# Query-key products placed behind the products with values, a full-height sample chunk, and one tile of high and low parts for the samples' output projection

## The chip, the cores and the metric

The kernel runs on one core of a Trainium2 chip. The metric is device time in microseconds (us), the median of several runs. The core has a matrix engine (TensorE, "PE" in the rows; "PEld" is its loading of weights), VectorE (DVE), ScalarE (ACT), GpSimd (POOL), and queues of memory transfers that are issued by SyncE (SP). The engines run side by side and wait for each other through semaphores. TensorE writes into PSUM, which has eight banks of 128 x 512 float32; the other engines read the results from there into the on-chip memory.

## The reference

One layer of a hybrid decoder trunk, for a prompt of 1024 tokens and for samples (8 sequences of 8 tokens, 64 tokens in all), all in float32:

```python
h = rmsnorm(x) * (1 + scale) + shift              # adaLN, from c
q, k, v, g_att, z, xbc, dt, g_a, g_b = split(h @ w_in)
for window, dilation in ((128, 1), (512, 4), (2048, 16)):
    o, lse = dilated_window_attention(q, k, v)    # 8 heads of 64, ALiBi; samples read a cache
att = combine(o, lse) * silu(g_att)
y = gated_rmsnorm(ssd(conv(xbc), dt) + d_skip * x, z)   # 32 heads of 64, state 128, chunks of 128
merged = sigmoid(g_a) * (att @ w_att_branch) + sigmoid(g_b) * (y @ w_ssm_branch)
out = rmsnorm(x + gate * (merged @ w_out))
```

It returns the new rows, the kept keys and values, and the states of the scan and of the convolution.

## The kernel before

Activations lie transposed (features on the partitions, 1088 tokens along them: 1024 of the prompt and then 64 of the samples). To keep float32 accuracy, the large products are made of three: an operand is split into a high part of type F32R and a low part (what is left), and a product is high x high, low x high and high x low (`mm3`, lines 195 to 200; `pj` in the rows is a PSUM tile of such a projection, of 352 or 368 columns).

The work has four stages. First come norm, modulation and two early projections. Then come the attention, the state-space branch, and the output.

In attention and state-space branch the order of TensorE's instructions is the order in which the program writes them. The projections are the main stream (`run`), and the attention or the scan is a second stream (`attention`, `side`), a generator that is advanced between groups of projection products whenever its due time by a running estimate has come (`order.spend`, `yield`). So each step of the attention is a short burst of products between projection products. The other engines' order is set by a scheduler when the kernel is built. In the output stage that scheduler also orders TensorE.

The attention of a prompt group (`prompt_group`, lines 590 to 679) works on a pair of heads at a time: head 0 on partitions 0 to 63, head 1 on partitions 64 to 127. There are 12 such groups (4 pairs of heads, 3 dilations). A group has `nb` blocks of queries, 4 for the first two dilations and 2 for the third. For each block there is

- `scores`: the query-key products into two PSUM tiles `s0`, `s1` (rows `s<-k,q`). They use 64 rows of the matrix engine, the two heads side by side (form `64*128` in the rows). Then VectorE adds the mask and takes the extreme value into `pr` (line 617), and ScalarE takes the exponent (line 620);
- `turned`: transposes of `pr` (rows `pt`, full array, form `128*128`), copied to `pT` by ScalarE and VectorE (lines 639, 641);
- `values`: products of `pT` with the values (rows `o<-pT,v`), 64 columns of the array for each head (form `128*64`).

A step `i` of the loop at line 663 issues `values(i - 2)`, then `turned(i - 1)`, then `scores(i)`. `pr` has one buffer; the two PSUM tiles of scores have two banks in all.

In the state-space branch (`x_tile`), the products within a chunk (`yd`, lines 1074 to 1084) run over eight chunks of 128 tokens and a ninth, of the 64 sample tokens, that uses 64 rows (form `64*64`). The mask `CB`, with which the decays `mt` are multiplied, has zeros on partitions 64 to 127 of the samples' columns already (line 937).

In the output stage (lines 1105 to 1223), the branches' products add up in `acc`; for each of the 8 feature blocks `m` the merged result is split into `mhi[m]` and `mlo[m]` (`split`). `ada_gate` makes the adaLN gate from eight tiles `wg`, which lie in the pool `yw`. The last loop, over `t`, takes 128 tokens at a time and the 64 samples as `t == 8`. For each half of the features (quarter for the samples) it makes 8 x 3 products into a bank (`fo`), and then VectorE multiplies by the gate and adds the residual (lines 1209, 1210), ScalarE sums the squares (1211), and VectorE multiplies by the norm's weight (1212). After the last part come the norm's factor and the store.

Of the kernel before, what the change touches and what calls it, by code (L numbers as in the profile page):

```python
# [9 lines left out]
F32 = mybir.dt.float32  # L10
F32R = mybir.dt.float32r
AF = mybir.ActivationFunctionType
OP = mybir.AluOpType
# [3 lines left out]
D = 1024  # L17
T = 1024
NB = 8
NS = 8  # L20
TS = NB * NS
TT = T + TS
KO = D // 128
# [87 lines left out]
def trunk(ctx: ExitStack, tc: tile.TileContext, I, O):  # L111
    nc = tc.nc
    V, S, G, PE, SP = nc.vector, nc.scalar, nc.gpsimd, nc.tensor, nc.sync
# [18 lines left out]
    bankA, bankB, bankC, bankPJ = bank("a"), bank("b"), bank("c"), bank("p")  # L132
# [73 lines left out]
    def mm(out, w, x, ns, **kw):  # L206
        PE.matmul(out, w, x, **kw)  # L207
        order.spend(ns)
# [248 lines left out]
        del gates[:n]  # L457
        return [job(j) for j in js]

    def ada_gate(pool_, k, pg):  # L460

        wg = pool_.tile([128, D], F32, tag="wg", name="wg", bufs=1)
        SP.dma_start(out=wg, in_=I["w_gate"][k])
        for j in range(4):
            PE.matmul(pg[j * 32:j * 32 + 32, :256], scT[:, k, :], wg[:, j * 256:(j + 1) * 256], start=k == 0, stop=k == 7)
        if k < 7:
            return
        gt = pool_.tile([128, 256], F32, tag="gt", name="gt", bufs=1)
        for j in range(4):
            SP.dma_start(out=gt[j * 32:j * 32 + 32], in_=bass.AP(tensor=I["b_gate"].tensor, offset=I["b_gate"].offset + j * 256,  # L470
                                                                 ap=[[0, 32], [1, 256]]))
        V.tensor_add(gt, gt, pg[:, :256])
        for j in range(4):
            SP.dma_start(out=gate_d[:, j * 256:(j + 1) * 256], in_=gt[j * 32:j * 32 + 9])
# [8 lines left out]
    with ExitStack() as actx:  # L483
# [106 lines left out]
        def prompt_group(hp, g, n, q, k, v, msk, o):  # L590


            w = 256 if g < 2 else 128
            per = 512 // w
            nb = 8 // per
            st = ap_.tile([128, 2, 2, 8], F32, tag="st", name="st")
            prs, pTs, pos = {}, {}, {}

            def behind(u):
                return 2 if (g == 0 and u > 0) or (g == 1 and u % 2 == 1) else 1  # L600

            def scores(i):
                us = range(i * per, i * per + per)

                ps = [bankA("s0"), bankA("s1")]
                for u in us:
                    nkb = behind(u)
                    c0, k0 = (u - us[0]) * w, (u + 1 - nkb) * 128
                    for h in range(2):
                        hs = slice(h * 64, h * 64 + 64)  # L610
                        mm(ps[h][:, c0:c0 + nkb * 128], q[hs, u * 128:(u + 1) * 128], k[hs, k0:k0 + nkb * 128], 110.0 * nkb,
                           start=True, stop=True)
                pr = prs[i] = ap_.tile([128, 2, 512], F32, tag="pr", name="pr", bufs=1)
                for u in us:
                    c0, m = (u - us[0]) * w, behind(u) * 128
                    for h in range(2):
                        V.tensor_tensor_reduce(out=pr[:, h, c0:c0 + m], in0=ps[h][:, c0:c0 + m], in1=msk[:, h, w - m:w],  # L617
                                               scale=-1.0, scalar=3e38, op0=OP.add, op1=OP.min,
                                               accum_out=st[:, 0, h, u:u + 1])
                        S.activation(pr[:, h, c0:c0 + m], pr[:, h, c0:c0 + m], AF.Exp, scale=-1.0,  # L620
                                     bias=st[:, 0, h, u:u + 1], accum_out=st[:, 1, h, u:u + 1])

            def turned(i):
                pr = prs.pop(i)
                pT = pTs[i] = ap_.tile([128, 8, 128], F32, tag="pT", name="pT", bufs=1)
                us = range(i * per, i * per + per)
                half = per // 2
                for x in range(2):
                    pt = bankB("pt").rearrange("p (x n) -> p x n", n=128)
                    y = 0  # L630
                    for u in us[x * half:x * half + half]:
                        nkb = behind(u)
                        for h in range(2):
                            for b in range(nkb):
                                c0 = (u - us[0]) * w + b * 128
                                turn(pt[:, y, :], pr[:, h, c0:c0 + 128], ident)
                                y += 1
                    if x:
                        V.tensor_copy(pT[:, 4:4 + y], pt[:, :y])  # L639
                    else:  # L640
                        S.activation(pT[:, :y], pt[:, :y], AF.Copy)

            def values(i):
                pT = pTs.pop(i)
                us = range(i * per, i * per + per)
                half = per // 2
                for x in range(2):
                    y = 4 * x
                    for u in us[x * half:x * half + half]:
                        if u % 4 == 0:  # L650
                            pos[0] = bankC("o")
                        po = pos[0]
                        nkb = behind(u)
                        for h in range(2):
                            for b in range(nkb):
                                mm(po[h * 64:h * 64 + 64, (u % 4) * 128:(u % 4 + 1) * 128],
                                   v[:, u + 1 - nkb + b, h * 64:h * 64 + 64], pT[:, y, :], 115.0,
                                   start=b == 0, stop=b == nkb - 1)
                                y += 1
                        if u % 4 == 3:  # L660
                            S.activation(o[:, (u - 3) * 128:(u + 1) * 128], po, AF.Copy)

            for i in range(nb + 2):
                if i > 1:
                    values(i - 2)
                if 0 < i <= nb:
                    turned(i - 1)
                if i < nb:
                    scores(i)
                if i == nb - 1:  # L670
                    order.passed.add(("s", n))
                if i <= nb:
                    order.spend(300)
                    yield (5500.0 if g < 2 else 7500.0),
            ps = bankB("stt")
            turn(ps[:32, :128], st.rearrange("p a h u -> p (a h u)"), ident)
            sr = ap_.tile([32, 128], F32, tag="sr", name="sr", bufs=1)
            V.tensor_copy(sr, ps[:32, :128])
            SP.dma_start(out=st_d[hp, g].rearrange("a h (u n) -> (a h u) n", n=128), in_=sr)
# [146 lines left out]
    with ExitStack() as bctx:  # L826
# [135 lines left out]
        def x_tile(gr, xt, Bk, Bs, CB, CT, CS, sq):  # L962
# [111 lines left out]
            for q in range(3):  # L1074
                ps = bankA("yd")
                w = 512 if q < 2 else TS
                if q == 2:
                    yield 2000.0,
                for c in range(4 * q, 4 * q + 4 if q < 2 else 9):
                    n = 128 if c < 8 else TS  # L1080
                    for h in range(2):
                        mm(ps[h * 64:h * 64 + 64, (c % 4) * 128:(c % 4) * 128 + n],
                           xdt[:n, c, h * 64:h * 64 + 64], mt[h][:n, c * 128:c * 128 + n], 115.0, start=True, stop=True)
                V.tensor_add(u[:, 512 * q:512 * q + w], u[:, 512 * q:512 * q + w], ps[:, :w])
            zs = tiles.pop(("z", xt))
            th = b1.tile([128, TT], F32, tag="ecs", name="th")
# [21 lines left out]
    with pool("yr", 2) as yr, pool("yw", 2) as yw:  # L1108
# [31 lines left out]
        for gr in range(5):  # L1140
# [9 lines left out]
            for m in range(8):  # L1150
                vhi, vlo, _ = load_w(I["w_ssm"][gr, m] if gr < 4 else I["w_att"][m], 4, 128, yw)
                if gr == 1:
                    ada_gate(yw, m, pg)
                if gr == 3:
                    raw = yr.tile([128, D], F32, tag="yx", name="wo")
                    SP.dma_start(out=raw, in_=I["w_out"][m])
# [19 lines left out]
                if gr == 4:  # L1176
# [2 lines left out]
                    mhi.append(a)  # L1179
                    mlo.append(b)  # L1180


    fp = ctx.enter_context(pool("fin", 1))
    f2 = ctx.enter_context(pool("fin2", 2))
# [6 lines left out]
    for t in range(9):  # L1191
# [6 lines left out]
        m = 2 if t < 8 else 4  # L1198
        w = D // m
        for i in range(m):  # L1200
            ps = bankA("fo")[:n, :w]
            cs = slice(i * w, (i + 1) * w)
            for k in range(KO):
                hi = mhi[k][:, t * 128:t * 128 + n]
                lo = mlo[k][:, t * 128:t * 128 + n]
                PE.matmul(ps, hi, whi[:, k, cs], start=k == 0, stop=False)  # L1206
                PE.matmul(ps, lo, whi[:, k, cs], start=False, stop=False)  # L1207
                PE.matmul(ps, hi, wlo[:, k, cs], start=False, stop=k == KO - 1)  # L1208
            V.tensor_tensor(y[:n, cs], ps, (gbs if t == 8 else gb)[:n, cs], op=OP.mult)
            V.tensor_tensor(y[:n, cs], y[:n, cs], x[:n, cs], op=OP.add)  # L1210
            S.activation(ps, y[:n, cs], AF.Square, accum_out=s[:n, 3 + i:4 + i])
            V.tensor_tensor(x[:n, cs], y[:n, cs], fg[:n, cs], op=OP.mult)
# [158 lines left out]
```

## Time and profile before

| | |
|---|---|
| median of 3 runs | 1911.06 us (1909.26 to 1911.51) |
| the profiled execution | 1912.37 us, its span 1910.6 us |
| TensorE busy | 1871.7 us (98% of the span) |
| VectorE busy | 1023.6 us (54%) |
| ScalarE busy | 665.1 us (35%) |
| GpSimd busy | 359.7 us (19%) |
| mean granted TensorE clock | 0.992 |

The span is the time from the first to the last instruction of the profiled execution. In the timelines a row is a run of equal instructions: start in us from the span's start, length in us, engine, line, operation, output<-inputs, the form and how often. Products are pipelined, and their lengths overlap; what tells the pace is the distance from one start to the next.

### The profile page before, as it was taken

To read this page: it belongs to the slowest core of one execution; us is meant where nothing else is said; L and a number is where in the kernel's file an instruction comes from. 1 tells how busy PE (TensorE), PEld (TensorE's weight loads), DVE (VectorE), ACT (ScalarE), POOL (GpSimd) and SP (SyncE) were. 2 spreads that over 40 slices of the span, in tenths; PEclk is the share of its full clock that TensorE was granted. 3 is DMA by queue.
4 is the path that set the end of the run, shared out by engine and by line. 5 is a ranking of instruction groups with operands and counts; after the bars stand their busy time and mean duration, and the time that the engine had idled before them with its cause. 6 is when DMAs were issued, how large, how long until landed. Compare 5 with 4: busy or idle time off the path is not lost.

```text
span 1910.6 us, 32219 instructions
## 1 busy us (share of the span) xinstructions
PE 1871.7 (98%) x13057; PEld 1747.7 (91%) x13057; DVE 1023.6 (54%) x1946; ACT 665.1 (35%) x1275; POOL 359.7 (19%) x576
## 2 busy tenths in 40 slices
PE   6999999999999999999999999999999999999998
PEld 4999989988998999999989998999898999999987
DVE  4633343325324322566675777577757666566654
ACT  4444233313423332424343435243434332131222
POOL 3100000000000000134513442444244300001300
PEclk8999999999999999999999999999999999999999
DMA  8422462273246227434443444444233364364322
GB/s 331 140 79 93 156 205 77 86 227 121 97 158 197 84 90 242 149 124 170 147 140 132 155 151 137 138 140 135 86 104 104 120 236 143 124 198 144 120 89 78
DMA packets 108949, 269.57 MB, mean 141 GB/s; under 512 B 41580, under 2 KB 50592, under 8 KB 105536
## 3 DMA queue, kind: packets, MB, share of 16 engines
q1 hardware_dynamic: 108800, 267.51, 42.3%
q8 instruction: 102, 1.67, 0.4%
q14 instruction: 47, 0.39, 0.1%
HBM read 224.93 MB, written 80.26 MB: 160 GB/s over the span
## 4 chain that ended last, share of the span: by engine, by line
PE 87%; DVE 5%; DMA 4%; ACT 2%; issue 1%; POOL 1%; SPq 0%; ACTq 0%; POOLq 0%; DVEq 0%
PE pj L198 22%; PE pj L199 21%; PE pj L200 21%; PE o L207 2%; PE pt L211 2%; PE s L207 2%; PE fo L1208 2%; PE fo L1206 2%; PE fo L1207 2%; PE yo L207 2%; DMA csb<-cs_d 2%; PE yd L207 2%; PE early L242 1%; PE stt L207 1%; PE tt L211 1%
## 5 line engine op out<-in xcount | busy, mean ns | idle before, releaser
L198 PE MATMUL pj<-h_hi,whi 128*128 128x368 f32 x2256 | 753.4, 334 | 0.0
L199 PE MATMUL pj<-h_hi,wlo 128*128 128x368 f32 x2256 | 738.4, 327 | 0.0
L200 PE MATMUL pj<-h_lo,whi 128*128 128x368 f32 x2256 | 738.4, 327 | 0.0
L198 PEld LDWEIGHTS pj<-h_hi,whi 128*128 128x128 f32 x2256 | 424.3, 188 | 25.5 <-issue 23.0
L199 PEld LDWEIGHTS pj<-h_hi,wlo 128*128 128x128 f32 x2256 | 424.6, 188 | 0.7
L200 PEld LDWEIGHTS pj<-h_lo,whi 128*128 128x128 f32 x2256 | 424.1, 188 | 0.0
L192 DVE TENSOR_TENSOR wlo<-wraw,whi 128x1024 fp32r<-128x1024 f32 (+1 forms) x136 | 151.0, 1110 | 204.9 <-ACT whi L191 203.0
L191 ACT ACTIVATE whi<-wraw 128x1024 fp32r<-128x1024 f32 (+1 forms) x136 | 126.5, 930 | 326.8 <-PE pj L200 262.5
L198 PE MATMUL pj<-yhi,whi 128*128 128x368 f32 (+1 forms) x480 | 157.7, 329 | 0.7 <-DVE acc L1170 0.7
L199 PE MATMUL pj<-yhi,wlo 128*128 128x368 f32 (+1 forms) x480 | 157.2, 327 | 0.0
L200 PE MATMUL pj<-ylo,whi 128*128 128x368 f32 (+1 forms) x480 | 156.9, 327 | 0.0
L620 ACT ACTIVATE pr<-pr,st 128x128 f32<-128x128 f32 (+1 forms) x192 | 83.9, 438 | 69.0 <-DVE st L617 68.9
L639 DVE COPY pT<-pt 128x512 f32<-128x512 f32 x40 | 27.6, 690 | 137.6 <-PE pt L211 64.0
L198 PEld LDWEIGHTS pj<-yhi,whi 128*128 128x128 f32 x480 | 90.1, 188 | 3.7 <-issue 2.1
L199 PEld LDWEIGHTS pj<-yhi,wlo 128*128 128x128 f32 x480 | 90.1, 188 | 1.5 <-issue 0.8
L200 PEld LDWEIGHTS pj<-ylo,whi 128*128 128x128 f32 x480 | 90.1, 188 | 0.0
L874 DVE SCALAR_TENSOR_TENSOR xc<-raw,cw,xc 128x1112 f32<-128x1112 f32 x60 | 82.5, 1375 | 12.3 <-ACT xc L872 11.5
L559 POOL COPY ks<-k 128x64 f32<-128x64 f32 x12 | 3.7, 306 | 379.2 <-DVE k L500 379.2
L1175 POOL TENSOR_TENSOR acc<-acc,ta 128x368 f32<-128x368 f32 (+1 forms) x24 | 24.2, 1009 | 249.2 <-DVE ta L1174 249.2
L969 DVE TENSOR_TENSOR csb<-tok,csb 128x2048 f32<-128x2048 f32 x16 | 39.6, 2477 | 55.3 <-DMA csb<-cs_d 55.3
L1002 POOL TENSOR_TENSOR xde<-xdt,tok 128x256 f32<-128x256 f32 x64 | 45.3, 734 | 115.9 <-DVE xdt L995 115.9
L500 DVE COPY k<-pj 128x368 f32<-128x368 f32 (+2 forms) x44 | 24.0, 581 | 75.0 <-PE pj L200 72.5
(269 smaller groups left out, 2596.6 us busy)
## 6 DMA issues: line engine op xcount, KB each, us to landing
wraw<-in_w_in SPq DMA_DIRECT2D x96, 512.0 KB, 4.4
csb<-cs_d SPq DMA_DIRECT2D x16, 1088.0 KB
kt<-in_kc SPq DMA_DIRECT2D x32, 448.0 KB, 4.6
out_kc<-in_kc SPq DMA_DIRECT2D x32, 448.0 KB, 5.0
out_vc<-in_vc SPq DMA_DIRECT2D x28, 512.0 KB, 4.7
vt<-in_vc SPq DMA_DIRECT2D x28, 512.0 KB, 5.5
sg_d<-sg SPq DMA_DIRECT2D x16, 544.0 KB, 2.7
ecs<-cs_d SPq DMA_DIRECT2D x32, 272.0 KB, 3.9
```

Of the source, the lines that this page charges most:

```text
L191: S.activation(hi, raw, AF.Copy)
L192: V.tensor_sub(lo, raw, hi.bitcast(F32))
L198: PE.matmul(ps, whi[:, k, :], xhi[k], start=first and k == 0, stop=False)
L199: PE.matmul(ps, wlo[:, k, :], xhi[k], start=False, stop=False)
L200: PE.matmul(ps, whi[:, k, :], xlo[k], start=False, stop=last and k == n - 1)
L207: PE.matmul(out, w, x, **kw)
L211: PE.transpose(out, x, eye)
L620: S.activation(pr[:, h, c0:c0 + m], pr[:, h, c0:c0 + m], AF.Exp, scale=-1.0, bias=st[:, 0, h, u:u + 1], accum_out=st[:, 1, h, u:u + 1])
L874: V.scalar_tensor_tensor(c, raw[:, t:t + CONV], cw[:, j, t:t + 1], c, op0=OP.mult, op1=OP.add)
L969: V.tensor_tensor(csb[:, :, :T].rearrange("p h (c l) -> p h c l", l=CH), tok[:, :8, 32 + h0:34 + h0].rearrange("p c h -> p h c")[:, :, :, ...
L1002: G.tensor_tensor(xde[:, c:c + 2].rearrange("p c (h d) -> p c h d", h=2), xdt[:, c:c + 2, :].rearrange("p c (h d) -> p c h d", h=2), tok[: ...
L1206: PE.matmul(ps, hi, whi[:, k, cs], start=k == 0, stop=False)
```

## The change

Three edits.

1. In `prompt_group`, `scores` is cut in two: the products stay in `scores`, and the mask, the extreme value and the exponents become `exponents`. A step now issues `values(i - 2)`, `scores(i)`, `turned(i - 1)`, `exponents(i)`.
2. In `x_tile`, the ninth chunk of `yd` uses all 128 rows; the upper 64 rows of `mt` hold zeros there.
3. In the output stage, the samples' columns of `mhi[m]` and `mlo[m]` are copied side by side into a tile `smp` (128 x 8 x 128) by ScalarE. For `t == 8`, eight products of `smp` with the high part of the weights give high x high on PSUM partitions 0 to 63 and low x high on partitions 64 to 127. ScalarE copies the latter to `low`, VectorE multiplies it by the gate and adds it to the residual `x`. Eight more products, of the high part with the low part of the weights, add to partitions 0 to 63. `smp` shares its place with `wg`, which moves from the pool `yw` to the pool `acp`.

```diff
-    def ada_gate(pool_, k, pg):
+    def ada_gate(pool_, wgp, k, pg):
-        wg = pool_.tile([128, D], F32, tag="wg", name="wg", bufs=1)
+        wg = wgp.tile([128, D], F32, tag="smp", name="wg")
...
-                ps = [bankA("s0"), bankA("s1")]
+                ps = sps[i] = [bankA("s0"), bankA("s1")]
...
+            def exponents(i):
+                us = range(i * per, i * per + per)
+                ps = sps.pop(i)
                 pr = prs[i] = ap_.tile([128, 2, 512], F32, tag="pr", name="pr", bufs=1)
...
             for i in range(nb + 2):
                 if i > 1:
                     values(i - 2)
+                if i < nb:
+                    scores(i)
                 if 0 < i <= nb:
                     turned(i - 1)
                 if i < nb:
-                    scores(i)
+                    exponents(i)
...
                         mm(ps[h * 64:h * 64 + 64, (c % 4) * 128:(c % 4) * 128 + n],
-                           xdt[:n, c, h * 64:h * 64 + 64], mt[h][:n, c * 128:c * 128 + n], 115.0, start=True, stop=True)
+                           xdt[:, c, h * 64:h * 64 + 64], mt[h][:, c * 128:c * 128 + n], 115.0, start=True, stop=True)
...
-                    ada_gate(yw, m, pg)
+                    ada_gate(yw, acp, m, pg)
...
+                    if m == 0:
+                        smp = acp.tile([128, KO, 2 * TS], F32R, tag="smp", name="smp")
+                    S.activation(smp[:, m, :TS], a[:, T:].bitcast(F32), AF.Copy)
+                    S.activation(smp[:, m, TS:], b[:, T:].bitcast(F32), AF.Copy)
...
-            ps = bankA("fo")[:n, :w]
+            ps = bankA("fo")
             cs = slice(i * w, (i + 1) * w)
-            for k in range(KO):
+            if t == 8:
+                for k in range(KO):
+                    PE.matmul(ps[:, :w], smp[:, k, :], whi[:, k, cs], start=k == 0, stop=k == KO - 1)
+                low = f2.tile([TS, w], F32, tag="low", name="low")
+                S.activation(low, ps[TS:, :w], AF.Copy)
+                V.tensor_tensor(low, low, gbs[:, cs], op=OP.mult)
+                V.tensor_tensor(x[:n, cs], x[:n, cs], low, op=OP.add)
+                for k in range(KO):
+                    PE.matmul(ps[:n, :w], smp[:, k, :TS], wlo[:, k, cs], start=False, stop=k == KO - 1,
+                              skip_group_check=True)
+            ps = ps[:n, :w]
+            for k in range(KO if t < 8 else 0):
```

More of the change, by code (lines that the diff above doesn't have):

```diff
@@ L596, in prompt_group @@
             st = ap_.tile([128, 2, 2, 8], F32, tag="st", name="st")
-            prs, pTs, pos = {}, {}, {}
+            sps, prs, pTs, pos = {}, {}, {}, {}
             def behind(u):
```

## The prediction

> **What bounds the kernel now.** I read the page first (engines, chain), then TensorE's waits, then its groups with the shapes kept apart, then timelines of single bursts.
>
> ```profile
> span 1910.6 us, 32219 instructions
> PE 1871.7 (98%) x13057; PEld 1747.7 (91%) x13057; DVE 1023.6 (54%) x1946; ACT 665.1 (35%) x1275; POOL 359.7 (19%) x576
> PE 87%; DVE 5%; DMA 4%; ACT 2%; issue 1%; POOL 1%; SPq 0%; ACTq 0%; POOLq 0%; DVEq 0%
> PE pt L211 <- ACT pr L620: 2.7, 3, 1.0
> PE cb L207 <- DVE CT L881: 2.5, 1, 2.5
> ```
>
> TensorE is busy for 98% of the span and holds 87% of the chain, so whatever shortens its stream ahead of the last stage moves the end. The waits named for it are small; the one on `pr` is touched by this change. "Busy" hides pace, though: lengths overlap, and a slower start-to-start distance inside a busy stretch is seen only in a timeline. This is one full step of the attention between projection products:
>
> ```profile
> 100.93 0.33 PE L200 MATMUL pj<-h_lo,whi 128*128 128x368 f32 x1
> 101.19 0.93 PE L207 MATMUL o<-pT,v 128*64 128x128 f32 x12
> 102.05 1.09 PE L211 MATMUL pt<-pack,pr 128*128 128x128 f32 x8
> 103.07 1.13 PE L207 MATMUL s<-k,q 64*128 64x256 f32 x8
> 104.14 0.44 PE L198 MATMUL pj<-h_hi,whi 128*128 128x368 f32 x1
> 104.41 0.33 PE L199 MATMUL pj<-h_hi,wlo 128*128 128x368 f32 x1
> 104.58 0.33 PE L200 MATMUL pj<-h_lo,whi 128*128 128x368 f32 x1
> ...
> 109.88 1.15 PE L207 MATMUL o<-pT,v 128*64 128x128 f32 x16
> 110.96 1.09 PE L211 MATMUL pt<-pack,pr 128*128 128x128 f32 x8
> ```
>
> The step uses three shapes of the array: 64 columns per head (`o`), the full array (`pt`), 64 rows (`s`), and then the full array again. Their paces: two projection starts in a row are 0.17 us apart (104.41, 104.58). Four more `o` make 1.08 instead of 0.86 us, so twelve should take 0.66. Two more bursts give the other paces:
>
> ```profile
> 760.59 0.33 PE L200 MATMUL pj<-h_lo,whi 128*128 128x368 f32 x1
> 760.76 0.39 PE L211 MATMUL soT<-pack,so 128*128 128x128 f32 x2
> 760.90 0.41 PE L198 MATMUL pj<-h_hi,whi 128*128 128x368 f32 x1
> 761.15 0.33 PE L199 MATMUL pj<-h_hi,wlo 128*128 128x368 f32 x1
> ...
> 143.93 0.33 PE L200 MATMUL pj<-h_lo,whi 128*128 128x368 f32 x1
> 144.10 0.82 PE L211 MATMUL pt<-pack,pr 128*128 128x128 f32 x6
> 144.84 0.93 PE L207 MATMUL s<-k,q 64*128 64x128 f32 x8
> 145.70 0.43 PE L198 MATMUL pj<-h_hi,whi 128*128 128x352 f32 x1
> 145.97 0.32 PE L199 MATMUL pj<-h_hi,wlo 128*128 128x352 f32 x1
> ```
>
> Two transposes between projections take 761.15 - 760.59 = 0.56 us with two projection paces (0.34) in it, thus 0.11 each, and nothing for going to them and back: both are full array. The `s` at 144.84 have four records of 128 columns (the row merges both shapes) and take 0.86 us; all eight of 256 columns take 1.07. Doubling two pairs adds 0.21, so a pair of heads takes 0.105 us per 128 columns. Now the full step, from 100.93 to 104.58: 3.65 us, of which 0.50 are three projection paces, 0.66 `o`, 0.88 `pt`, 0.84 `s`. The 0.77 us left are four changes of shape, 0.19 each.
>
> **The change part by part.** *Scores ahead of the transposes.* The step becomes projection, `o`, `s`, `pt`, projection; from `pt` back to projections no shape changes. Four changes become three. This holds where a step has all three, at i = 2 and 3 of the two dilations with four blocks: 4 for each pair of heads, 16 in all: 16 x 0.19 = 3.1 us. No row shows `o` followed directly by `s`. If the direct change costs what the two that it replaces cost (0.38), the gain is 0; if it were free, 6.2. I take the mean of the four that are shown.
>
> At i = 1 there are `pt` and `s` alone (three per pair of heads, 12 in all). From 143.93 to 145.97 are 2.04 us: two projection paces 0.33, six `pt` 0.66, `s` 0.63, and 0.42 for two changes. After there are two as well, into `s` and from `s` to `pt`, and the projection's late second start (0.27 for 0.17 us) goes; `pt` behind another shape loses a little less (1.02 - 0.88 = 0.14 on both of its sides together). I take 0.04 each, 0.5 us, with 0 to 1.3 as bounds.
>
> *Waits in these steps.* The dearest wait on `pr` is in the first steps behind a combination of heads:
>
> ```profile
> 437.26 0.27 PE L211 MATMUL pt<-pack,pr 128*128 128x128 f32 x1
> 437.59 0.41 DVE L617 CUSTOM_DVE_ANT_0 pr<-s,msk 128x256 f32<-128x256 f32 x1
> 438.53 0.93 PE L211 MATMUL pt<-pack,pr 128*128 128x128 f32 x5 [1.00 <-ACT pr L620]
> ```
>
> TensorE loses 1.27 - 0.11 = 1.16 us here. With `s` in front it will wait for something else: both score banks must be free, which is when VectorE's last reduction ends, 437.59 + 0.41 = 438.00, so 0.74 is lost and 0.42 gained; the exponents end under the new `s`. Of three such places (2.7 us in the waits view) I take 1.0 us together, bounds 0 and 2.7. In the other steps scores now come at the place where `pt` stood and need the reductions only, which end ahead of the exponents. The new order delays the exponents: `pr` is free only behind the last transpose, and VectorE copies `pT` first. But `pt` comes later by the 1.07 us of `s`, so nobody waits longer; the evacuations of projections queued behind them on ScalarE and VectorE move by under 1 us against three projection banks that TensorE takes 24 x 0.17 = 4.1 us each to fill. Cost 0. No transfer is moved.
>
> *The ninth chunk at full height.* Two pairs of products per tile, 16 tiles:
>
> ```profile
> 889.81 0.33 PE L207 MATMUL yd<-csb,xdt 64*64 64x64 f32 x4
> 890.07 0.43 PE L198 MATMUL pj<-h_hi,whi 128*128 128x368 f32 x1
> ...
> 810.90 0.33 PE L207 MATMUL cb<-CTs,xcs 128*64 128x64 f32 x2
> 811.16 0.44 PE L198 MATMUL pj<-h_hi,whi 128*128 128x368 f32 x1
> ```
>
> The shape goes from `64*64` to `128*64`, still not that of the projections on both sides, so two changes stay two. 128 rows and 64 columns (`cb`) end as soon behind their start (0.26 us) as the low form. I take 0, bounds 0.8 us either way (16 x 0.05). The zeros are there already, so no instruction is added.
>
> *The samples' output projection.* 96 products become 64:
>
> ```profile
> 1891.20 0.28 PE L1206 MATMUL fo<-wohi,yhi 128*64 128x256 f32 x1
> 1891.40 0.69 DVE L1209 TENSOR_TENSOR fy<-fo,gb 128x512 f32<-128x512 f32 x1 [3.46 <-PE fo L1208]
> 1895.15 0.42 DVE L1212 TENSOR_TENSOR fx<-fy,fg 64x256 f32<-64x256 f32 x1
> 1895.50 0.15 DVE L158 TENSOR_TENSOR fs<-fs 128x1 f32<-128x1 f32 x1
> 1896.06 0.49 DVE L1222 TENSOR_SCALAR fy<-fx,fs 128x512 f32<-128x512 f32 x1
> 1902.50 0.28 PE L1208 MATMUL fo<-wolo,yhi 128*64 128x256 f32 x1
> 1902.83 0.42 DVE L1209 TENSOR_TENSOR fy<-fo,gbs 64x256 f32<-64x256 f32 x1 [1.27 <-PE fo L1208]
> 1903.28 0.42 DVE L1210 TENSOR_TENSOR fy<-fy,fx 64x256 f32<-64x256 f32 x1
> ```
>
> 95 distances from 1891.20 to 1902.50 are 0.119 us each, so 32 products fewer are 3.8 us of TensorE. But VectorE gets eight more operations of 64x256, in a stage where it was waiting for TensorE only 1.27 us a quarter. Ahead of the last residual addition (1903.28) it has, counted from 1891.40: what is left of `t == 7` (three of 0.7 and one of 0.49, seven small ones), two small sums, and ten, now eighteen, of 64x256. An independent one follows after 0.35 us (1895.15 to 1895.50), a dependent one after 0.45 (1902.83 to 1903.28). With 0.35: 2.15 + 0.49 + 9 x 0.12 + 18 x 0.35 = 10.0, so 1901.4 instead of 1903.28: 1.9 us gained. With 0.45 throughout: 11.8, gain nil. If TensorE alone set the end: 3.8. VectorE has two quarters' work to interleave, so I take 1.9. The second eight products must wait if they may not write while ScalarE reads the same bank; the next quarter's first eight stand ready to fill that.
>
> The Trainium skill, page "TensorEngine Tiling (Array Packing)", section "PSUM Bottleneck", says that packing speeds up the matrix engine and not the emptying of PSUM. By that rule the tail gains what VectorE allows (sum 6.5 us below); by TensorE's pace alone the sum would be 8.4. The row's 1.27 us of VectorE idling per quarter against eight added operations agrees with the rule.
>
> *Copies into `smp`.* Sixteen on ScalarE, of 128x64:
>
> ```profile
> L859 ACT ACTIVATE raw<-pj 128x64 f32<-128x64 f32 x24 | 5.3, 221 | 0.0
> 1558.00:1801.60 243.60, 242.86 (x1489) 236.81 (x1487) 150.21 (x207) 54.33 (x68) 22.30 (x23) 1.00 0.47 155
> ```
>
> 16 x 0.22 = 3.5 us beside a stage in which ScalarE (fifth figure) is busy for 54 of 244 us: 0. If the copies of the last blocks got in front of the last splits, up to 1.3 us (six of them) at the loop's start. `wg` changes its place and not its transfers: 0.
>
> **Sum:** 3.1 + 0.5 + 1.0 + 1.9 = 6.5 us less. The profiled execution took 1912.37 us (1910.6 of span and 1.8 around it), 1.3 above the median of 1911.06. Median after: 1904.6 us. A difference under 0.2%, 3.8 us, can't be told from none by this measurement: faster means under 1907.2.
>
> **The rivals.** *Tail set by TensorE alone*: VectorE's idle time, 1.27 us a quarter, speaks against it; 1.9 more gives 1902.7. Chance 0.1.
>
> *Tail gains nothing*, VectorE's operations all at the dependent distance: 1906.5. For it speaks that its order is fixed at build and each part's operations depend on each other; against it that small ones slot in between before. 0.15.
>
> *The loss is in the shape, not in the change of it*: `s` may be slow at its start wherever it stands, and from `o` to `s` both rows and columns change. Then the direct change costs two, part one gives the 1.5 of the lesser terms at most, and with the tail it is 1907.7: no difference that can be told. 0.14.
>
> *Slower*: a direct change from column to row tiles that costs far more than any shown. It decides from 0.19 + (6.5 + 3.8) / 16 = 0.83 us a step; at 0.9 us the time is 1916. The four shown, 0.19 on average, speak against it. The Trainium skill's "TensorEngine Tiling (Array Packing)", "Key Properties", counts one drain per change of mode, which is against it as well; no row here shows this pair. 0.06.
>
> *Stalls elsewhere*: TensorE's waits in the state-space branch (2.5 us at `cb` alone) hang on the other engines' order, which is made anew at each build; one such wait more gives 1907.1, one less 1902.1. This widens the likeliest case.
>
> **How the numbers follow.** The sum holds with 0.55, between 1901.5 and 1907.2. Faster: 0.55 + 0.1 + half of the second rival = 0.72. Same: the other half, the third rival = 0.21. Slower: 0.07, 0.06 of it the fourth rival. The range, 1900.8 to 1909.8, reaches over the third rival with one wait more, and to the first with one wait less.
>
> **What would show it.** In the profile after, a full step's burst should go `o`, `s`, `pt` and be shorter by 0.19 us, with the projection right behind `pt` (0.03 and 0.25 us); `o` to `s` should be near 0.2 above the pace. `pt <- pr` should leave the waits and `s <- pr` come, smaller. In the tail, 64 products at 0.119, and VectorE without its idle 1.27 us. I am wrong if bursts keep their length, if the last `fo` ends 3.8 us earlier and the end does not follow by about 2, or if a wait in the state-space branch moves by more than the sum.

## The result, and the profile after

The changed kernel takes 1899.11 us (median of 4 runs, 1898.54 to 1899.8) against 1910.51 beside it (4 runs): 0.9941 of the time before, 95% interval 0.9926 to 0.9955. Two later comparisons of the same two programs gave 0.9945 (0.9931 to 0.9959) and 0.9939 (0.9919 to 0.9958). So the change saves about 11 us, where 6.5 were forecast; the direction was right, and the time lies 1.7 us under the range. (One execution of e12_ahead below, 4634.77 us with projection products 0.425 instead of 0.168 us apart, is left out of every figure.)

The page of the profile after (share of the span and number of instructions of each engine):

```profile
span 1898.0 us, 32246 instructions
PE 1862.4 (98%) x13025; PEld 1741.8 (92%) x13025; DVE 1021.8 (54%) x1954; ACT 670.1 (35%) x1295; POOL 357.7 (19%) x576
```

TensorE lost 32 instructions and 9.3 us of busy time, VectorE won eight instructions and ScalarE twenty. Some of TensorE's waits after, in the state-space branch (us in total, times, longest):

```profile
PE yo L207 <- DVE sta L1035: 3.5, 3, 1.2
PE ms L165 <- POOL raw L857: 2.1, 1, 2.1
PE cb L207 <- DVE CT L888: 1.0, 2, 0.5
```

The 2.7 us of `pt <- pr` are gone, and no wait of `s` stands in the list. That list needs care, as the first bursts will show. TensorE's timeline of a full step, of a step at i = 1, and of a first step behind a combination of heads:

```profile
101.16 0.32 PE L200 MATMUL pj<-h_lo,whi 128*128 128x368 f32 x1
101.42 0.93 PE L207 MATMUL o<-pT,v 128*64 128x128 f32 x12
102.27 1.14 PE L207 MATMUL s<-k,q 64*128 64x256 f32 x8
103.34 1.09 PE L211 MATMUL pt<-pack,pr 128*128 128x128 f32 x8
104.19 0.41 PE L198 MATMUL pj<-h_hi,whi 128*128 128x368 f32 x1
104.44 0.33 PE L199 MATMUL pj<-h_hi,wlo 128*128 128x368 f32 x1
104.61 0.34 PE L200 MATMUL pj<-h_lo,whi 128*128 128x368 f32 x1
...
143.75 0.33 PE L200 MATMUL pj<-h_lo,whi 128*128 128x368 f32 x1
144.01 0.93 PE L207 MATMUL s<-k,q 64*128 64x128 f32 x8
144.87 0.87 PE L211 MATMUL pt<-pack,pr 128*128 128x128 f32 x6
145.50 0.40 PE L198 MATMUL pj<-h_hi,whi 128*128 128x352 f32 x1
145.74 0.32 PE L199 MATMUL pj<-h_hi,wlo 128*128 128x352 f32 x1
...
435.26 0.32 PE L200 MATMUL pj<-h_lo,whi 128*128 128x352 f32 x1
435.51 1.83 PE L207 MATMUL s<-k,q 64*128 64x256 f32 x8
435.73 0.41 DVE L621 CUSTOM_DVE_ANT_0 pr<-s,msk 128x256 f32<-128x256 f32 x1
436.21 0.73 PEld L207 LDWEIGHTS s<-k,q 64*128 64x128 f32 x6 [0.41 <-DVE st L621]
437.27 0.88 PE L211 MATMUL pt<-pack,pr 128*128 128x128 f32 x6
437.90 0.41 PE L198 MATMUL pj<-h_hi,whi 128*128 128x352 f32 x1
```

The full step takes 104.61 - 101.16 = 3.45 us from one `L200` product to the next, instead of 3.65. From the last `o` to the first `s` are 0.20 us, as long as before from `o` to `pt` and again from `pt` to `s`. So the direct change costs one change, not two. (The forecast had 0.2 above the pace at this one place. It is 0.1, and the second pair of `s` adds the other 0.1: it comes 0.31 us behind the first, where 0.21 is usual.) The step at i = 1 takes 1.99 instead of 2.04 us. In the first step `s` lasts 1.83 us where 1.14 is usual: about 0.7 us are lost inside a run of instructions that counts as busy, so the list of waits does not show them. The weight loads' row does: they wait for VectorE's last reduction (L621), as forecast.

The tail, with the last products and VectorE's work on the samples:

```profile
1881.32 3.02 PE L1219 MATMUL fo<-wohi,smp 128*128 128x256 f32 x24
1881.51 0.69 DVE L1234 TENSOR_TENSOR fy<-fo,gb 128x512 f32<-128x512 f32 x1 [3.46 <-PE fo L1233]
1884.17 1.08 PE L1225 MATMUL fo<-wolo,smp 128*64 128x256 f32 x8
1885.09 1.12 PE L1219 MATMUL fo<-wohi,smp 128*128 128x256 f32 x8
1886.04 2.89 PE L1225 MATMUL fo<-wolo,smp 128*64 128x256 f32 x24
1887.40 0.41 DVE L1234 TENSOR_TENSOR fy<-fo,gbs 64x256 f32<-64x256 f32 x1
1887.74 0.41 DVE L1223 TENSOR_TENSOR fx<-fx,low 64x256 f32<-64x256 f32 x1
1888.07 0.14 DVE L159 TENSOR_SCALAR fs<-fs 128x1 f32<-128x1 f32 x1
1888.13 0.41 DVE L1234 TENSOR_TENSOR fy<-fo,gbs 64x256 f32<-64x256 f32 x1
1890.38 0.41 DVE L1235 TENSOR_TENSOR fy<-fy,fx 64x256 f32<-64x256 f32 x1
```

The order of TensorE's products was written quarter by quarter; the scheduler put the first eights of three quarters in a row (x24), then the second eight of one, the last quarter's first eight, and the three second eights that are left, so TensorE does not stand and wait for ScalarE's reading of a bank. VectorE's operations of 64x256 follow each other at 0.34 us without a wait for `fo`.

To see where time goes in every kernel, I cut the span by starts of TensorE's products: the attention from the first `dt` to the last `soT`; from there through the state-space branch and the merging to the first `fo`; then 89.6 us of prompt tokens in every kernel of the table; and the tail from the first `fo` of the samples to the end of the span. Before these come 61.5 to 63.6 us of norm and modulation.

| us, one profiled execution each | attention | state-space to `fo` | tail |
|---|---|---|---|
| before; again (e0_before) | 697.9; 698.8 | 1040.7; 1038.1 | 19.4; 19.4 |
| after; again (after2, e15_after) | 691.3; 691.4, 692.9 | 1036.8; 1043.5, 1038.2 | 16.7; 16.7, 16.7 |
| e1_scores | 692.0 | 1035.8 | 19.4 |
| e2_fullheight | 697.8 | 1044.3 | 19.4 |
| e3_tail | 697.6 | 1037.2 | 16.7 |
| e4_i1; e5_i2 | 696.4; 695.2 | 1038.8; 1037.2 | 19.4; 19.4 |
| e6_pool; e7_nolow | 692.1; 693.0 | 1035.8; 1040.2 | 18.0; 15.9 |
| e10_wg | 698.8 | 1040.4 | 19.4 |
| e8_join; e9_join64 | 692.9; 692.3 | 1044.3; 1043.5 | 16.7; 16.7 |
| e14_behind (e11_behind); e13_ahead | 692.4 (691.6); 692.0 | 1036.7 (1036.9); 1034.5 | 16.7; 16.7 |

The attention and the tail changed in every kernel that has their edit and in no other. The middle moves by 6.7 us between executions of one and the same program (after). Waits that come and go are only half of this. From the trace of after2, behind one such wait (in the last row the third figure from the end is the granted clock of TensorE in that stretch):

```profile
970.22 1.11 PE L165 MATMUL ms<-sq,onesc 128*32 128x272 f32 x2 [2.19 <-POOL sq L1106]
973.19 0.49 PE L198 MATMUL pj<-h_hi,whi 128*128 128x352 f32 x1
973.48 0.49 PE L199 MATMUL pj<-h_hi,wlo 128*128 128x352 f32 x1
...
972.00:975.00 3.00, 3.00 (x12) 3.00 (x12) 0.77 (x1) 2.95 (x4) 0.00 (x0) 0.50 0.62 151
```

The products come 0.29 us apart where 0.16 is usual, at half the clock, for 6.8 us in all; about half of that is lost (an estimate from these distances). Such periods, of 3.4 or 6.8 us, stand in the middle of most of these executions, near waits but not at each wait (none at one of 2.12 us at 1159.0 in after2): 6.8 us together in after, 13.7 in after2, none in e15_after. TensorE's idle time in the middle is 9.8, 13.1 and 13.4 us in these three. With the idle time and half of the periods taken off, the middle is 1023.5 to 1024.8 us in all thirteen executions from before to e10_wg in the table, with or without the edits.

### The profile page after: what moved, and what is told of

Read it like the earlier page. It is cut to its first block, busy times and chain, and to the rows that moved or that the text cites. A ratio compares the mean times of both kernels' runs of the same rounds, so it can differ in the third digit from the quotient of the medians.

```text
span 1898.0 us, 32246 instructions
## 1 busy us (share of the span) xinstructions
PE 1862.4 (98%) x13025; PEld 1741.8 (92%) x13025; DVE 1021.8 (54%) x1954; ACT 670.1 (35%) x1295; POOL 357.7 (19%) x576
## 5 line engine op out<-in xcount | busy, mean ns | idle before, releaser
L200 PE MATMUL pj<-h_lo,whi 128*128 128x368 f32 x2256 | 738.0, 327 | 0.0
L200 PEld LDWEIGHTS pj<-h_lo,whi 128*128 128x128 f32 x2256 | 423.8, 188 | 0.0
L200 PE MATMUL pj<-ylo,whi 128*128 128x368 f32 (+1 forms) x480 | 157.1, 327 | 0.0
L200 PEld LDWEIGHTS pj<-ylo,whi 128*128 128x128 f32 x480 | 90.1, 188 | 0.0
L881 DVE SCALAR_TENSOR_TENSOR xc<-raw,cw,xc 128x1112 f32<-128x1112 f32 x60 | 82.5, 1374 | 13.0 <-ACT xc L879 12.4
```

The lines of the kernel that those rows point to most:

```text
L200: PE.matmul(ps, whi[:, k, :], xlo[k], start=False, stop=last and k == n - 1)
L881: V.scalar_tensor_tensor(c, raw[:, t:t + CONV], cw[:, j, t:t + 1], c, op0=OP.mult, op1=OP.add)
```

## The experiments

### The three edits one by one, and the kernel before again

The kernel before, unchanged; then each edit alone, as in the diff above.

> The kernel before once more, for a second profile. If TensorE's waits in the state-space branch belong to the order in which the other engines' instructions stand, they come back where they were: about 2.5 us at cb near 993, 2.1 us at ms near 1161, 2.1 us at ms near 1347, three of about 1.2, 1.2 and 0.7 us at yo between 1439 and 1478, and the time is 1910 to 1912 us. If they are chance, each moves by more than 1 us or goes, and no stage of the kernel before can be compared with one of the kernel after below some 3 us.

> Only the first edit (scores ahead of the transposes). Theory A: besides the 3.1 us of saved changes of shape and about 2.8 us in the steps at i = 1 (their waits), this edit also makes the scheduler order VectorE, ScalarE and SyncE otherwise in the state-space branch, and 2 to 3 us of waits at cb and ms go there: 1901.5 to 1903 us, with the waits at cb and ms as in the kernel after. Rival B, the state-space gain belongs to another edit or to chance: 1904 to 1905.5 us, and cb keeps its 2.5 us.

> Only the second edit (the ninth chunk of yd at 128 rows). Theory A: no instruction changes its place and the shape changes cost as before; no difference, 1910 to 1912 us, and four yd records between projections take 0.45 to 0.47 us over the projections' pace as before. Rival B, the state-space gain comes from this edit: 1907 to 1908.5 us.

> Only the third edit (smp). Theory A: the end of TensorE comes 3.8 us earlier and the end of the kernel 2.7 us, since VectorE has eight operations more; with half a microsecond or so in the rest of the output stage: 1907 to 1908.5 us, and the state-space branch keeps its waits. Rival, the tail follows TensorE: 1906.5 us or less. Rival B, the state-space gain comes from this edit: 1904.5 to 1906 us.

Measured: the kernel before again 1909.57 us (one run). Edit 1 alone 1903.53 us, ratio 0.9963 (0.9949 to 0.9977). Edit 2 alone 1912.66, ratio 1.0004 (0.9994 to 1.0014). Edit 3 alone 1906.56, ratio 0.998 (0.9966 to 0.9994). On the time before of some 1911 us these are 7.1 less, no difference, and 3.8 less: together 10.9, as much as the change brings. Edit 3's tail is 2.7 us shorter, as its theory A had it. In the second execution of before TensorE's waits are not where they were: one of 2.1 us at `ms` is gone, and the 2.5 us at `cb` are two, of 1.5 and 1.2.

Edit 1 gains in the attention; its middle stretch, 1035.8, is low, but the kernel before has 1038.1 in one of its executions and e4_i1, with nearly the new order, 1038.8, so my theory that edit 1 brings a better order to the state-space branch has nothing that stands out of the spread. Its time lies between the two theories' ranges and does not decide. Edit 2 leaves the instructions of all engines in their places; the burst of the ninth chunk loses 464 ns on the projections instead of 457: no gain.

### Which steps of the attention

Edit 1 alone, with the scores ahead only where `ahead` holds:

```diff
+                ahead = i == 1        # e4_i1; e5_i2: i > 1
                 if i > 1:
                     values(i - 2)
-                if i < nb:
+                if i < nb and ahead:
                     scores(i)
                 if 0 < i <= nb:
                     turned(i - 1)
                 if i < nb:
+                    if not ahead:
+                        scores(i)
                     exponents(i)
```

> The first edit in the steps at i = 1 alone (12 of them); the others keep their order. The stage from the dt products to the last soT takes 697.6 to 698.8 us without the first edit and 691.3 to 692.0 with it. Theory A: these 12 steps give 2.8 us, 0.5 of it shapes and 2.3 waits on pr that become shorter waits or none: 695.0 to 695.6 us. Rival: here too the shapes make the gain, 12 x 0.045 = 0.5 us, and what waited on pr waits on the score banks: 697.2 us or more. The whole span can't tell it, since the state-space stage varies by 6 us on its own.

> The first edit in all steps but those at i = 1: 16 steps with all three products. Theory A, one change of shape of 0.19 us less in each: the stage from the dt products to the last soT takes 694.6 to 695.3 us, every full burst is 0.195 us shorter, and the three waits on pr of 0.7 to 1.0 us stay. Rival, the direct change from o to s costs two: no burst is shorter. With the run at i = 1 it tells whether the two sum to the 6.4 us of the whole edit.

Measured: 1907.66 and 1905.59 us (one run each). A burst's loss is the time from the last projection product ahead to the third behind, less the projections' own pace. Summed over all bursts against the kernel before, e5_i2 loses 3.07 us less, all in the 16 full steps (0.19 each); e4_i1 loses 2.78 less, in the 12 steps at i = 1. Eight of these 12 give 0.045 each. The other four, the first steps of a head pair, lose (in the changed kernel) 1.88, 2.55, 2.57 and 2.55 us instead of 2.42, 3.01, 3.31 and 3.28: 2.5 us, of which the change of shape is 4 x 0.045 and the rest, 2.3, waits. The whole attention tells the two edits' shares less well: 695.2 us for e5_i2, as expected, and 696.4 for e4_i1 where 695.0 to 695.6 were, while the kernel before itself moved by 0.9. The places with waits were four and not three: one of them, at 92.87 us before, does not stand in TensorE's list of waits, only in the weight loads' rows of the timeline of before:

```profile
92.87 1.32 PE L211 MATMUL pt<-pack,pr 128*128 128x128 f32 x6
93.25 0.31 PEld L211 LDWEIGHTS pt<-pack,pr 128*128 128x128 f32 x3 [0.41 <-ACT pr L620]
93.75 0.20 PEld L211 LDWEIGHTS pt<-pack,pr 128*128 128x128 f32 x2 [0.18 <-ACT pr L620]
```

Six transposes last 1.32 us there where 0.87 is usual. With the scores in front, no row there waits for `pr`.

### VectorE in the tail

In the changed kernel, the two operations on `low` on GpSimd (e6_pool), or left out (e7_nolow: the product of the samples' low parts is then not added):

```diff
-                V.tensor_tensor(low, low, gbs[:, cs], op=OP.mult)
-                V.tensor_tensor(x[:n, cs], x[:n, cs], low, op=OP.add)
+                G.tensor_tensor(low, low, gbs[:, cs], op=OP.mult)          # e6_pool
+                G.tensor_tensor(x[:n, cs], x[:n, cs], low, op=OP.add)
```

> The kernel after, with the two added operations of each samples' quarter (low times gate, plus residual) on GpSimd instead of VectorE. From the first product of the samples to the end are 19.4 us before and 16.7 after. Theory A, VectorE's occupancy sets the tail after: 15.0 to 15.9 us, the last PE start to the end back towards 8.1 to 8.6 us from 9.37. Rival, the chain through low and the residual sets it: 16.7 us or more, as GpSimd's operations are slower. The whole time moves by about 1 us, too little for its interval.

> The kernel after without those two operations at all: the low part's product is made and copied, but not added to the samples' result. Theory A: the tail follows TensorE, 19.4 - 3.97 = 15.4 us from the first product of the samples to the end, 8.1 us from the last start. Rival, something else than the added VectorE work holds the tail (the scheduler's order, ScalarE's copies): 16 us or more.

Measured: e6_pool 1902.39 us, ratio 0.9945 (0.9921 to 0.997), not told apart from the changed kernel; e7_nolow 1902.78 (one run). The tails tell more: 16.7 us as changed, 15.9 without the eight operations, 18.0 with them on GpSimd. TensorE's last product starts 7.34 us into the tail, and the kernel before needed 8.09 from there to the end, so by TensorE alone it would be 15.4. The tail is 1.3 us over that, of which leaving out the eight operations gives back 0.85, not all as expected; in e7_nolow an operation of VectorE on another quarter (at 1893.31) still stands between the reading of the last product and its addition. The theory that a VectorE with less to do ends the tail at 15.0 to 15.9 us failed for e6_pool. GpSimd's timeline there, with ScalarE and VectorE ahead of the last copy:

```profile
1882.77 0.73 POOL L1222 TENSOR_TENSOR low<-low,gbs 64x256 f32<-64x256 f32 x1 [87.64 <-ACT low L1221]
1884.62 1.55 POOL L1222 TENSOR_TENSOR low<-low,gbs 64x256 f32<-64x256 f32 x2
1887.08 0.69 DVE L160 TENSOR_TENSOR fs<-fs 128x1 f32<-128x1 f32 x1
1887.85 0.72 ACT L1245 ACTIVATE fy<-fx,fs 128x512 f32<-128x512 f32 x1
1888.48 0.36 ACT L1221 ACTIVATE low<-fo 64x256 f32<-64x256 f32 x1
1888.89 1.15 PE L1225 MATMUL fo<-wolo,smp 128*64 128x256 f32 x8 [1.01 <-ACT low L1221]
```

An operation that takes VectorE 0.34 us from start to start takes GpSimd about 0.75. The last quarter's `low` is copied only at 1888.48, and TensorE, which must not write the bank before, waits 1.0 us for it: its last product starts 8.59 us into the tail. On ScalarE this copy stands behind the scaling of the last prompt tokens (L1245), which needs VectorE's norm factor (L160). That small operation takes 0.69 us here and 0.14 in the changed kernel, and other operations of VectorE beside GpSimd's are longer too (1.23 instead of 0.68 us at L1237). So the end is set by a chain over three engines, and slower operations of VectorE beside GpSimd's are part of it; that GpSimd causes them is not shown.

### The place of wg

All kernels with edit 3 (but e8_join and e9_join64 below, with 31.0) have 23.65 us instead of 24.31 between the last `ms` of the state-space branch and the first product of the output stage, which looked like a gain. The kernel before, with `wg` moved as in the change and nothing else:

> The kernel before, with nothing of the change but the place of wg (in the pool of acc instead of yw, eight tiles' turns as before). All kernels with the third edit have 23.65 us instead of 24.31 between the last product of the state-space branch (ms) and the first product of the output stage. Theory W (where wg lies lets the first weights of the output stage come earlier, or moves the gate's products): 23.65 us here too, and the tail as before (19.4 us from the first product of the samples to the end). Rival S (the copies into smp or the new order of the last loop do it): 24.31 us. The time itself, with 1908 to 1912, tells nothing.

Measured: 1912.91 us (one run), and 23.65 us. The first expectation holds, and it is no gain: the `gate` products only moved. In the kernel before the first eight of them (0.64 us) lie directly ahead of the output stage's first product, at 1556.31; after the change they start some 50 us behind it. First start and last stand in the answers on that line, of before and after:

```profile
L465 PE MATMUL gate<-wg,scT x64: 379/391/403, 1555.7 to 1652.6; 128*32 128x256 f32 x64
...
L465 PE MATMUL gate<-wg,scT x64: 379/391/403, 1595.5 to 1643.4; 128*32 128x256 f32 x64
```

### The ninth chunk joined to the eight

If a change of shape costs 0.19 us, the second edit opens a larger gain than its own: with all nine chunks in one shape, the ninth need not stand alone between projections. In the changed kernel:

```diff
-                ps = bankA("yd")
+                ps = (bankA if q < 2 else bankB)("yd")
...
-                if q == 2:
-                    yield 2000.0,
```

e9_join64 has the ninth chunk at 64 rows again.

> The changed kernel with the ninth chunk of yd joined to the other eight: the break in the stream before q == 2 is gone, and the third PSUM tile comes from the other group of banks. The ninth chunk then costs only its own four products beside others of its shape. Theory P (every change of shape costs about 0.19 us, and the ninth chunk alone between projections pays two of them): 16 tiles x 2 x 0.19 = 6 us less, with the late second projection start gone as well; the joined burst loses about 2.3 us on the projections instead of 2.09 + 0.46; the time is 1893 to 1894 us. Rival Q (the ninth chunk's break hides a wait: products without it must wait for VectorE to add the first two tiles or for a bank): the joined burst is as long as the two were, or TensorE gets new waits at yd, and the time stays at 1898 to 1901.

> The kernel with the joined ninth chunk, with the second edit undone: the ninth chunk's products use 64 rows again, so the form within the joined burst changes from 128*64 to 64*64. Theory P (a change of shape is what costs): one change more in each of 16 bursts, 16 x 0.19 = 3 us slower than the joined one at full height, so 1896 to 1897. Rival R (fewer rows within the same columns cost nothing, since the second edit alone brought nothing): as the joined one at full height, within 1 us.

> The changed kernel once more, for the comparison on the same chip with the joined one, and to see which stages of the same program move: the attention within 0.2 us of 691.3, the tail within 0.1 of 16.7, the state-space branch anywhere between 764 and 772, the time 1898 to 1903.

Measured: e8_join 1903.26 us, ratio 0.9955 (0.9941 to 0.997); e9_join64 1904.02, 0.9964 (0.9949 to 0.9978); the changed kernel on that chip 1900.62, 0.9945 (0.9931 to 0.9959). Joining made it slower, if anything. A joined burst and TensorE's largest waits in e8_join:

```profile
878.09 0.32 PE L200 MATMUL pj<-h_lo,whi 128*128 128x368 f32 x1
878.34 2.08 PE L207 MATMUL yd<-csb,xdt 128*64 128x128 f32 x36
880.35 0.43 PE L198 MATMUL pj<-h_hi,whi 128*128 128x368 f32 x1
...
PE ms L165 <- POOL sq L1104: 9.0, 4, 2.3
PE tt L211 <- DVE xc L888: 7.0, 4, 3.0
```

The bursts kept their promise: a tile's products lose 2.195 us on the projections instead of 2.086 + 0.464, and over 16 tiles, those with transposes behind included, 5.0 us less. But the changed kernel has 0.8 us of waits for `xc` and 0 to 4.3 for `sq`; here they are 16. Others became fewer: TensorE's idle time in the whole middle is 19.9 us, instead of 9.8 to 13.4 in the three executions of the changed kernel. Neither expectation named this: the wait is not at `yd` but at the parts that follow, which come 2 us earlier by their due times than the other engines are ready. With 64 rows the joined burst loses 2.351 us alone and 3.287 instead of 3.213 with the transposes behind it, 0.07 to 0.16 a tile: 1.8 us in all, smaller than the 3 expected, and the two times do not differ by what the intervals can tell. The changed kernel's attention and tail, 691.4 and 16.7 us, are as expected; its state-space branch (here from the last `soT` to the last `ms`), 773.6 us, is above the 764 to 772 that were.

The break kept, behind the products (`yield 2000.0` after the loop) or ahead of them (`yield 8000.0` for 6000):

> The kernel with the joined ninth chunk, with the break of 2000 put behind the products with xdt instead of ahead of the ninth chunk, so that whatever follows comes as late as in the changed kernel. Theory Y (the lost break let the next part of the stream come too early and made TensorE wait for POOL and VectorE): the bursts keep the 5 us that the join brought, the waits for sq and xc fall back from 16 us to 2 to 5 us, and the time is 1894 to 1897. Rival Z (these waits come with any other order or by chance, the break has no part in it): waits of 10 us or more stay, 1900 to 1904.

> The same with the break put ahead: the due time ahead of all products with xdt is 8000 instead of 6000. The eight chunks come 2 us later than in the changed kernel, the ninth as late as there. Theory Y: as with the break behind, 1894 to 1898, with perhaps one wait more for sq, since VectorE's additions of the first two tiles come later. Rival Z: 1900 to 1904.

> The joined ninth chunk with the break of 2000 ahead of all products with xdt, beside the changed kernel on the same chip. Theory Y (the join saves 5 us of bursts and the kept break holds off the waits that ate them): 3 to 6 us less than the changed kernel, the joined burst loses 2.2 us on the projections, the wait for xc is under 1 us. Rival Z (the waits come with any new order): less than 2 us of difference.

> The joined ninth chunk with the break behind, on the same chip. Theory Y: 3 to 5 us less than the changed kernel; its waits for sq, 7.7 us in the execution seen, are back at 2 to 5 us if they came by chance, at 7 to 9 if the order makes them. Rival Z: less than 2 us of difference.

> The changed kernel on the same chip as the two with the joined chunk: 1899 to 1901, 0.994 of the time before; attention 691.3 to 691.4 and tail 16.7 as in the two executions seen, the state-space branch between 764 and 774.

Measured, first chip: behind 1897.64 us, ratio 0.9923 (0.9908 to 0.9938); ahead 1895.85, 0.9918 (0.9901 to 0.9934). Second chip, with the changed kernel: ahead 1897.08, 0.9912 (0.9895 to 0.9928); behind 1896.74, 0.9909 (0.989 to 0.9928); the changed kernel 1902.17, 0.9939 (0.9919 to 0.9958). The two are 5.1 and 5.4 us faster by the medians (6 runs each; the means differ by 5.2 and 5.1, with standard errors of 1.3 and 1.5), which is what the bursts save. So the lost break had turned the gain into waits: with it back in either place, TensorE's idle time in the middle is 12.4 to 13.7 us again. (The changed kernel's time and attention, 692.9 us, were a little longer here than expected.) TensorE's waits with the break ahead, then behind:

```profile
PE ms L165 <- POOL sq L1104: 4.8, 5, 2.1
PE tt L211 <- DVE xc L888: 0.6, 1, 0.6
...
PE ms L165 <- POOL sq L1105: 7.6, 6, 2.1
PE tt L211 <- DVE xc L888: 0.7, 1, 0.7
```

`xc` is back where it was. The waits for `sq` with the break behind were 7.7 us in the one execution and 7.6 in the other, six times in both, more than the 2 to 5 us that theory Y had for `sq` and `xc`: these come with the order, not by chance, and the kernel wins in spite of them. These versions beat both kernels. With idle time and half-clock periods taken off as above, the middle is 1016.7 to 1018.7 us in the joined kernels at full height, some 6 us less than in the others.

## Why the prediction was right or wrong

*Full steps, 3.1 us*: right. 16 bursts lost 3.08 us less, the direct change from `o` to `s` costs one change (0.20 us from start to start), and the rivals that priced it at two or at 0.83 us fell. The Trainium skill's rule on the drain ("TensorEngine Tiling (Array Packing)", "Key Properties": changing the mode drains the engine, changing the tile does not) agrees with this 0.20, for which it has no price.

*Steps at i = 1, 0.5 us*: right, 12 x 0.045 = 0.54.

*Waits on `pr`, 1.0 us*: too small; 2.3 measured. The mechanism was read rightly: about 0.7 us are left to lose behind the change, as worked out from VectorE's last reduction. Three things made the term too small. Three times the worked 0.42 was rounded down to 1.0, by 0.26. The place that was read lost about 1.4 us and not 1.16, with a second wait of 0.18 in its weight loads' rows, and so did one more; these two gave 0.7 each, and only the third gave 0.42. And the fourth place, in the weight loads' rows alone, was not seen: it gave 0.5.

*The ninth chunk, 0*: right by itself (ratio 1.0004).

*The tail, 1.9 us*: 2.7 measured. The rule was right: VectorE, not TensorE, sets this end, so neither the rival with 3.8 nor the one with nothing came. From the first `fy` of the last prompt tokens to the last residual addition, 10.0 us were forecast and 8.87 measured (1890.38 - 1881.51): the operations follow at 0.34 us, most small ones add about 0.07 us where 0.12 was taken, and one operation of 64x256 and two small ones fewer lie ahead of that addition.

*Copies into `smp`, and `wg`, 0*: right.

With the measured terms the sum is 3.1 + 0.5 + 2.3 + 2.7 = 8.6 us, and the prediction would have read 1902.5. So the step that failed is the size of these two terms, the waits on `pr` and the tail: 2.1 us of the 5.5 that were missing. The rest lies in the middle stretch, which the sum put at 0. There the forecast put the waits down to the order that is made anew at each build, and allowed for one such wait of 2.5 us. This step failed too: the changed program itself took 1036.8, 1043.5 and 1038.2 us in that stretch, waits come and go with nothing changed, and the half-clock periods, 0 to 6.8 us of loss, were not in the forecast at all. These are TensorE's rows for `cb` in the second execution of before (one wait of 2.5 us in the first) and for `sq` in the second of after (none in the first):

```profile
PE cb L207 <- DVE CT L881: 2.7, 2, 1.5
...
PE ms L165 <- POOL sq L1106: 4.3, 2, 2.2
```

The middle stretch had to be taken as uncertain by some 3 us either way without any change to it. Chance from one execution to the next is still not all of the rest. The three comparisons, weighted by their intervals, give 11.1 us saved, 9.4 to 12.8, and 8.6 lies outside. As the middle's work without idle time and half-clock loss is the same in all thirteen executions, a steady gain there would have to be fewer of these. Together they cost 16.9 us on average in the four executions without edits 1 and 3 (13.7 to 20.4), and 14.0 in the nine with one of them or both (11.1 to 19.9). The ranges overlap, so whether the edits bring this about, and how, stays open.

## What to carry to other kernels

On an engine that is never idle, count the changes of shape in its stream and price one from start-to-start distances between neighbours; here that price held to a hundredth of a microsecond in 16 places. Look for lost time inside runs that count as busy, and in the weight loads' rows, before adding up a list of waits, and read the granted clock behind the waits. And when a piece is joined to its neighbour, keep the pause that it made: the pause may be what lets the other engines finish (with it 5 us were won here, without it none).

## What the runs showed of the hardware unexpectedly

The 128-row, 64-column form of the ninth chunk saves nothing where it stands alone, and 0.07 to 0.16 us where it follows the same form directly, less than the 0.19 of a change to and from the full array. Waits of 1 to 2 us come and go between executions of one program, and with some of them come 3.4 or 6.8 us at half the granted clock. Both together moved a stretch of 1040 us by 6.7; without them it stayed within 1.3 us. An elementwise operation of 64x256 takes GpSimd 0.73 to 0.8 us (once 1.07) and VectorE 0.34 from start to start, and operations of VectorE that ran beside GpSimd's lasted up to 1.23 instead of 0.68 us (128x512) and 0.69 instead of 0.14 (128x1).
